# Hymba diffusion step on one core: an earlier gate row, a PSUM tile for each half of tile 8's last columns, separate norms of tiles 6 and 7, and a one-input softmax maximum

## Chip, cores and metric

The kernel runs on one core of one Trainium2 chip. The time is the device time in microseconds of one execution of the program; a kernel's time is the median of its runs. Engines are named as in the profile: PE (TensorE, matmuls), PEld (its weight loads), DVE (VectorE), ACT (ScalarE), POOL (GpSimd), SP (SyncE, which here issues DMAs). DMAs are issued from the queues of SP, ACT and POOL.

## What is computed

One step of a hybrid trunk with one layer, D = 1024, for 1024 latent tokens (with 256 cached context keys) and a prompt of 128 tokens. Cut to what matters here:

```python
def _block_attention(q_nope, q_ropes, key_sets):          # per head, per 128 query rows
    ...
        s = jnp.concatenate(logits, axis=-1).astype(jnp.float32) * ATTN_SCALE   # 1024 latent + 256 context keys
        p = jax.nn.softmax(s, axis=-1)
        return jnp.einsum('bhqk,bkhv->bqhv', p, v_all)

def _back(x, gate, a_out, attn, g_b, w_o):
    y = jnp.concatenate([a_out, attn * jax.nn.silu(g_b)], axis=-1) @ w_o
    return x + gate * y

    y_prompt = _rmsnorm(xp, final_g)
    y_sample = _rmsnorm(xs, final_g)
```

The mixer's other group (a gated MLP) and the input projections lie ahead of this and are not touched.

## The kernel before

Rows are worked on in nine tiles of 128: tiles 0 to 7 are the latent tokens, tile 8 the prompt. A product in fp32 is made of three matmuls on split numbers: each operand x has a rounded part (hi) and the rest x - hi (lo). The hi block is a copy with a cast on ACT or POOL, the lo block a subtraction on DVE (`lo_of`, L112).

**Attention.** For each tile t and head h, `softmax(t, h, ...)` takes the row maximum m over the 1024 latent logits (L1481) and over the 256 context logits (L1484), makes `nb`, the bias of the exponential, as max times `nscl` (L1485), the exponentials on ACT (L1491), and 1/sum (L1495, L1496); POOL multiplies (L1497). `value_stream` then works in steps of 512 columns: PE transposes e into `pT` (L1558), ACT writes its hi part `ph` (L1562), DVE its lo part `pl` (L112), and PE adds three matmuls each into `o` (L1582 to L1584); ACT copies `o` (L1592), PE multiplies by the value weights (`at`, L1601), DVE multiplies into `mixB` (L1603). Each engine runs its instructions in program order. `later(d, fn)` puts a piece of work d microseconds of an estimated clock later in that order.

**Work that rides along.** The output weights W_o are split (`wo_piece`), and weight sums T1 to T4 are formed in 16 `units`, each with a POOL subtraction of `traw` (L809), and stored to DRAM. The lists `his` and `los` hold split jobs, of which `spare_hi` and `spare_lo` issue a few after each softmax head and each `pl`. `t_fetch(3, n, ...)` loads the four T3 blocks back from DRAM (from POOL's queue, into the memory of split weights); `early_split(2)` issues the split of the third ring block, ringC; `wo_need(k)` issues whatever the k-th weight block still needs.

**Output projection.** Latent tiles go in pairs (0,1), (2,3), (4,5), (6,7), each a 2x2 block product in Strassen-Winograd form: seven products A11, A12, A22 and S1 to S4, with right sides B11, B21, B22, T1 to T4. Their left operands lie in rings of hi and lo blocks, ringA (in `area`), ringB and ringC. Three products of the first pair, in PSUM banks f0, f1, f2, and the prompt's right 512 columns (w8) are begun during the last attention heads (`early`); what is left of them is in `rest`. PE then goes through the products in the order S2, S3, S1, A11, ... (`products`). DVE combines their banks: c11, then m11, the multiplication of the first pair's columns by the gate row (L2195), u2, u4 and so on.

**The last part's order** is written by `Plan`, a list scheduler: steps have an engine, a cost, a priority (low first), what they wait for, and what they take and give back (PSUM banks "w", raw tiles). `fetch` chains loads one behind the other, cost 1.35. `load_gate` (L2048) loads the latent gate row as 128x1024, `load_own` the prompt's, `load_xr` (L1991) the residual x. For each group of tiles `norm` makes the sum of squares, a square root, a reciprocal with a correction, and the scaling by final_g: tile 6 on DVE (L2120), tile 7 in halves on POOL (L2132) and ACT (L2128). Last comes tile 8's left half: `left` makes columns 0 to 256 and 256 to 512 in one PSUM tile (`pz0`, `pz1`, 24 matmuls each); for each half DVE multiplies by the gate (`zm`, L2273) and adds x (`za`, L2274), ACT squares (`sq8.0`, `zq`), then follow zv, the root zr, rlast, and the output scaling: `out0` (DVE, left columns, SP's queue) and `out1` (ACT, right columns, ACT's queue).

Of the kernel before, what the change touches and what calls it, by code (L numbers as in the profile page):

```python
# [9 lines left out]
F32 = mybir.dt.float32  # L10
# [3 lines left out]
AF = mybir.ActivationFunctionType  # L14
ALU = mybir.AluOpType
# [3 lines left out]
P = 128  # L19
# [75 lines left out]
def tile_hymba_step(ctx: ExitStack, tc: tile.TileContext, I, O):  # L95
# [1375 lines left out]
    def softmax(t, h, lat_, con_):  # L1471

        m = sm.tile([P, 2], F32, tag="m", name=f"m{t}{h}", bufs=3)
        nb = sm.tile([P, 1], F32, tag="nb", name=f"nb{t}{h}", bufs=3)
        su = sm.tile([P, 2], F32, tag="su", name=f"su{t}{h}", bufs=3)
        rs = sm.tile([P, 1], F32, tag="rs", name=f"rs{t}{h}", bufs=3)
        e = ap_.tile([P, 1280], F32, tag="e", name=f"e{t}{h}", bufs=6)
        es[t, h] = e

        def start():  # L1480
            V.tensor_reduce(m[:, 0:1], lat_, axis=AX.X, op=ALU.max)  # L1481

        def shift():
            V.tensor_reduce(m[:, 1:2], con_, axis=AX.X, op=ALU.max)  # L1484
            V.scalar_tensor_tensor(nb, m[:, 0:1], m[:, 1:2], nscl[:, t : t + 1], op0=ALU.max, op1=ALU.mult)  # L1485
# [298 lines left out]
    with tc.manual_schedule(engines=engines):  # L1784
# [208 lines left out]
        def plain(k):  # L1993
            out_terms(8, wps[8], 512, 1024, [k])
            if k == 3:
                at_ = sum(1 for fn in his if rank.get(fn, 1) < 1)
                his[at_:at_] = [lambda n=n: t_fetch(3, n, woh[n][:, 512:1024], wol[n][:, 512:1024]) for n in range(4)]

        early = [(0.65, lambda k=k: plain(k)) for k in range(4)]
        early += [(0.65, lambda k=k: product(0, first_banks[0], ks=[k])) for k in range(4)]  # L2000
# [1 line left out]
            early.append((0.65, lambda k=k: plain(4 + k)))  # L2002
            early.append((0.65, lambda k=k: product(1, first_banks[1], ks=[k])))
        early += [(0.65, lambda k=k: product(2, first_banks[2], ks=[k])) for k in range(3)]
        later(6.0, lambda: (wo_need(4), early_split(2)))
        later(2.0, lambda: [t_piece(2, n, flat[2][2 + n]) for n in range(4)])
        vs = value_stream(pairs[-2])
        merged(vs[:3], [])
# [38 lines left out]

    def load_gate():  # L2048
        gate[0] = ep.tile([P, 1024], F32, name="gate0", tag="gate0")
        nc.scalar.dma_start(  # L2050
            gate[0].rearrange("p (j r) -> p j r", j=4), gdram.rearrange("j (c r) -> c j r", c=2)[0:1].broadcast_to([P, 4, 256])
        )

# [2 lines left out]
    def load_own(i, dma):  # L2056
# [2 lines left out]
        dma(t_[:, 0:512].rearrange("p (j r) -> p j r", j=2), rows.broadcast_to([P, 2, 256]))  # L2059
        dma(t_[:, 512:1024], I["x"][8][:, 512 * i : 512 * i + 512])  # L2060

    for m, n in ((1, 0), (4, 4)):
        for k in range(4):
            fetch(f"T{m}{k}", lambda m=m, k=k, n=n: t_piece(m, k, tpiece[n + k]))
        if m == 1:
            fetch("gate0", load_gate)
    fetch("own1", lambda: load_own(1, nc.scalar.dma_start))
    for t in (0, 1):
        fetch(f"x{t}", lambda t=t: load_xr(t))
# [7 lines left out]
        used[0] += n  # L2077
        return smalls[:, c : c + n]

    groups = {t: g for g in ((8,), (0, 1), (2, 3), (4, 5), (6, 7)) for t in g}  # L2080

    def square(t, j, junk, c, deps, prio=3.0, src=None):
        g = groups[t]
# [91 lines left out]
    def pair(n):  # L2175
# [24 lines left out]
        if True:  # L2200
# [56 lines left out]
    def finish_left():  # L2257
        v, v0, root, u = (small(1) for _ in range(4))
        r = sm.tile([P, 1], F32, tag="fr", name="rlast")
        cell = {}  # L2260
        fetch("own0", lambda: load_own(0, nc.sync.dma_start), ["y4"])
        g, x = (lambda: own[0][:, 0:512]), (lambda: own[0][:, 512:1024])
        on_g("z4", lambda: G.tensor_tensor(keep, keep, fg[:, R], op=ALU.mult), ["sq8.1", "fg"], 2.5)

        def left(j, c):
            if j == 0:
                cell["o"] = psw.tile([P, 512], F32, tag="w", name="left")
                cell["junk"] = psw.tile([P, 512], F32, tag="w", name="junk")
            out_terms(8, cell["o"][:, c], c.start, c.stop, range(8))

        for j, c in enumerate((slice(0, 256), slice(256, 512))):
            on_t(f"pz{j}", 2.9, lambda j=j, c=c: left(j, c), [], takes=("w", "w") if j == 0 else ())
            on_v(f"zm{j}", lambda c=c: V.tensor_tensor(cell["o"][:, c], cell["o"][:, c], g()[:, c], op=ALU.mult), [f"pz{j}", "own0"], 0.5, 0.42)  # L2273
            on_v(f"za{j}", lambda c=c: V.tensor_tensor(cell["o"][:, c], cell["o"][:, c], x()[:, c], op=ALU.add), [f"zm{j}"], 0.5, 0.42)  # L2274
        square(8, 0, lambda: cell["junk"][:, 0:256], L, ["za0"], 0.5, lambda: cell["o"][:, 0:256])
        sums((8,), v0, 0.5)
        on_v("zv1", lambda: V.tensor_scalar(v0, v0, 1.0 / 1024.0, EPS, op0=ALU.mult, op1=ALU.add), ["n8"], 0.5, 0.16)
        on_s(
            "zq", lambda: S.activation(cell["junk"][:, 256:512], cell["o"][:, 256:512], AF.Square, accum_out=ssq[(8,)][:, 2:3]), ["za1"], 0.4, 0.6
        )  # L2280
        on_v("zv", lambda: V.scalar_tensor_tensor(v, ssq[(8,)][:, 2:3], 1.0 / 1024.0, v0, op0=ALU.mult, op1=ALU.add), ["zq", "zv1"], 0.4, 0.2)
        on_s("zr", lambda: S.activation(root, v, AF.Sqrt), ["zv"], 0.3, 0.25)
        on_v("zr0", lambda: V.reciprocal(r, root), ["zr"], 0.3, 0.18)
        on_v("zr1", lambda: V.scalar_tensor_tensor(u, v, -0.5, r, op0=ALU.mult, op1=ALU.mult), ["zr0"], 0.3, 0.18)
        on_v("zr2", lambda: V.tensor_tensor(u, u, r, op=ALU.mult), ["zr1"], 0.3, 0.18)
        on_v("zr3", lambda: V.scalar_tensor_tensor(r, u, 1.5, r, op0=ALU.add, op1=ALU.mult), ["zr2"], 0.3, 0.18)

        def out0():
            V.scalar_tensor_tensor(x(), cell["o"], r, fg[:, L], op0=ALU.mult, op1=ALU.mult)
            nc.sync.dma_start(O["y"][8][:, L], x())  # L2290
# [116 lines left out]
```

## Time and profile before

| | |
|---|---|
| runs (us) | 624.31, 625.5, 625.46; median 625.46 |
| the profiled execution | 624.43 us, of it 622.7 us of span |
| granted TensorE clock, mean | 0.989 |
| PE, DVE, ACT, POOL busy | 96%, 69%, 53%, 34% |
| DMA | 67.33 MB, 108 GB/s over the span |

The span is the time from the profile's first instruction to its last. The page gives busy time by engine, the chain of work that ended last, and groups of instructions by line; a row of the timeline is start, duration, engine, line, operation, `out<-in`, shape, and in brackets the idle time before it with what ended it. A duration of a DVE row overlaps the next row's start by about 0.08 us; matmul durations include the way through the array, so the distance between starts is what one costs. A row of waits is who waited for whom: us in total, times, longest. In a row of the chain stand start, duration and what ran. DMA groups give KB of each transfer and the median us from issue to landing.

### The profile page before, as it was taken

Reading aid. Unit: us, or ns where it says so; the run is one execution under the profiler, and the core shown is the slowest. Engines: PE = TensorE matmul, PEld = TensorE weight load, DVE = VectorE, ACT = ScalarE, POOL = GpSimd, SP = SyncE. Lnnn points to the kernel's source line nnn. Section 1 sums busy time; section 2 is a strip of 40 time slices with the busy share of each in tenths; the row PEclk is TensorE's granted clock in tenths of the full one; section 3 lists DMA queues with packets and bytes.
Section 4 is the critical chain, followed back from the end, with each engine's and each line's share of the span. In section 5 each row is a group of like instructions: output and inputs, shape, how many; then the busy total and the mean of one; then the engine's idle time right before and its main releaser. Section 6 shows DMA issues by size and latency. Waiting matters only on the chain.

```text
span 622.7 us, 10205 instructions
## 1 busy us (share of the span) xinstructions
PE 599.6 (96%) x3671; PEld 540.6 (87%) x3671; DVE 427.5 (69%) x909; ACT 329.6 (53%) x763; POOL 209.2 (34%) x254
## 2 busy tenths in 40 slices
PE   7999999999999999999999999999999999799992
PEld 7678889999989999999988998899999888588882
DVE  4683458897755567566778677768777755368874
ACT  6556754336423345455676556665655542456642
POOL 2561111000000000333363354535344565179721
PEclk8999999999999999999999999999999999989997
DMA  8992010101261044000020143334411056932442
GB/s 321 390 376 69 1 34 2 35 1 54 100 237 65 21 119 131 14 1 1 2 74 1 35 136 121 126 128 135 133 72 35 1 201 196 369 113 77 157 139 101
DMA packets 32082, 67.33 MB, mean 108 GB/s; under 512 B 3472, under 2 KB 18592, under 8 KB 31520
## 3 DMA queue, kind: packets, MB, share of 16 engines
q1 hardware_dynamic: 27344, 54.88, 25.5%
q0 software_dynamic: 2880, 8.39, 4.1%
q10 hardware_dynamic: 1808, 3.41, 1.6%
q8 instruction: 29, 0.48, 0.3%
q14 instruction: 21, 0.17, 0.1%
HBM read 53.45 MB, written 13.21 MB: 107 GB/s over the span
## 4 chain that ended last, share of the span: by engine, by line
PE 80%; DVE 10%; ACT 4%; DMA 3%; issue 2%; SPq 0%; ACTq 0%
PE p L954 10%; PE tp L752 8%; PE tp L976 5%; PE pT L1558 4%; DVE pl L112 3%; PE zacc L1390 2%; PE zacc L1389 2%; PE zacc L1391 2%; PE s L1512 2%; PE s L1514 2%; PE s L1513 2%; PE s L1511 2%; PE s L1515 2%; DMA gate<-gdram 2%; PE o L1584 2%
## 5 line engine op out<-in xcount | busy, mean ns | idle before, releaser
L1497 POOL TENSOR_SCALAR e<-e,rs 128x1280 f32<-128x1280 f32 x32 | 46.9, 1466 | 100.4 <-ACT ph L1562 60.4
L112 DVE TENSOR_TENSOR pl<-pT,ph 128x512 fp32r<-128x512 f32 x81 | 55.4, 687 | 36.2 <-ACT ph L1562 34.5
L1491 ACT ACTIVATE e<-s,nb,scl 128x256 f32<-128x256 f32 x64 | 56.1, 880 | 41.0 <-DVE nb L1485 41.0
L1562 ACT CAST ph<-pT 128x512 fp32r<-128x512 f32 x80 | 46.3, 587 | 35.6 <-PE pT L1558 34.0
L1237 POOL TENSOR_TENSOR kr<-z,rope 128x64 f32<-128x64 f32 x8 | 2.6, 323 | 171.9 <-ACT z L1246 171.9
L752 PE MATMUL tp<-area,w 128*128 128x384 f32 x288 | 52.5, 338 | 0.0
L1558 PE MATMUL pT<-ident,e 128*128 128x128 f32 x320 | 48.4, 274 | 3.3 <-DVE pl L112 3.1
L752 PEld LDWEIGHTS tp<-area,w 128*128 128x128 f32 x288 | 50.4, 188 | 0.4
L1582 PE MATMUL o<-ph,vh 128*128 128x256 f32 x160 | 47.6, 298 | 0.0
L1584 PE MATMUL o<-ph,vl 128*128 128x256 f32 x160 | 45.0, 281 | 0.0
L1583 PE MATMUL o<-pl,vh 128*128 128x256 f32 x160 | 45.0, 281 | 0.0
L1558 PEld LDWEIGHTS pT<-ident,e 128*128 128x128 f32 x320 | 37.0, 140 | 8.1 <-PE at L1601 2.8
L1481 DVE TENSOR_REDUCE m<-s 128x1 f32<-128x1024 f32 x32 | 38.9, 1217 | 1.5 <-PE s L1515 1.5
L1511 PE MATMUL s<-kch,area 128*128 128x512 f32 (+2 forms) x100 | 39.1, 391 | 0.0
L1512 PE MATMUL s<-kcl,area 128*128 128x512 f32 (+2 forms) x100 | 35.3, 353 | 0.0
L1514 PE MATMUL s<-krh,area 128*128 128x512 f32 (+2 forms) x100 | 35.3, 353 | 0.0
L1513 PE MATMUL s<-kch,area 128*128 128x512 f32 (+2 forms) x100 | 35.2, 352 | 0.0
L1515 PE MATMUL s<-krl,area 128*128 128x512 f32 (+2 forms) x100 | 35.2, 352 | 0.0
L976 PE MATMUL tp<-area,w 128*128 128x384 f32 x192 | 35.0, 337 | 0.0
L976 PEld LDWEIGHTS tp<-area,w 128*128 128x128 f32 x192 | 33.6, 188 | 0.4 <-issue 0.4
L1583 PEld LDWEIGHTS o<-pl,vh 128*128 128x128 f32 x160 | 30.2, 189 | 1.4
L1582 PEld LDWEIGHTS o<-ph,vh 128*128 128x128 f32 x160 | 30.1, 188 | 1.4
(664 smaller groups left out, 1726.9 us busy)
## 6 DMA issues: line engine op xcount, KB each, us to landing
ada<-in_ada_ss SPq DMA_DIRECT2D x16, 512.0 KB, 8.1
w2r<-in_w_t SPq DMA_DIRECT2D x12, 512.0 KB, 4.4
x<-in_x SPq DMA_DIRECT2D x9, 512.0 KB, 7.2
adag<-in_ada_g SPq DMA_DIRECT2D x4, 1024.0 KB, 4.8
traw<-in_w_o SPq DMA_DIRECT2D x16, 256.0 KB, 3.7
tdram<-thi SPq DMA_DIRECT2D x32, 128.0 KB, 1.9
tdram<-traw SPq DMA_DIRECT2D x32, 128.0 KB, 1.9
wor<-in_w_o SPq DMA_DIRECT2D x8, 512.0 KB, 4.1
```

The lines of the kernel that those rows point to most:

```text
L112: V.tensor_tensor(lo, src, f32(hi), op=ALU.subtract)
L752: T.matmul(tps[i, g][:, :GW], w_[i][:, k, :], x_[k, g], start=k == 0 and j == 0, stop=k == NK - 1 and j == 2)
L954: T.matmul(banks[key], a_, b_, start=k == 0 and m == 0, stop=k == 3 and m == len(passes) - 1)
L976: T.matmul(tps[c, 2][:, :GW], w_[c][:, k, :], x_[k, 2], start=k == 0 and m == 0, stop=k == NK - 1 and m == 2)
L1491: S.activation(e[:, sl], src, AF.Exp, bias=nb, scale=scl[:, t : t + 1], accum_out=su[:, i : i + 1])
L1511: T.matmul(ps, qh_, kch[:, sl], start=True, stop=False)
L1512: T.matmul(ps, qh_, kcl[:, sl], start=False, stop=False)
L1514: T.matmul(ps, qr_, krh[:, sl], start=False, stop=False)
L1558: T.transpose(ps[:, w : w + P], es[t, h][:, c * P : (c + 1) * P], ident)
L1582: T.matmul(o, vh[:, kt, :], ph[:, sl], start=c == 0, stop=False)
L1583: T.matmul(o, vh[:, kt, :], pl[:, sl], start=False, stop=False)
L1584: T.matmul(o, vl[:, kt, :], ph[:, sl], start=False, stop=c == n - 1)
```

## The change

Four edits. (1) The reduction to `nb` has one input: a `tensor_reduce` over both columns of m and a `tensor_scalar` in place of a `scalar_tensor_tensor`, while `units` or `his` still hold work; that is so for 20 of the 32 heads. (2) The gate row is the first fetch of the last part and goes to SP's queue; the T3 loads go to the end of `his`, and `early_split(2)` is due at 0.5 instead of 6.0, without `wo_need(4)`. (3) Tiles 6 and 7 are two groups with norms of their own, at priority 0.45. (4) The two halves of tile 8's left columns have a PSUM tile each, and `out0` is two operations.

```diff
@@ softmax, shift() @@
-            V.scalar_tensor_tensor(nb, m[:, 0:1], m[:, 1:2], nscl[:, t : t + 1], op0=ALU.max, op1=ALU.mult)
+            if units or his:
+                V.tensor_reduce(nb, m, axis=AX.X, op=ALU.max)
+                V.tensor_scalar(nb, nb, nscl[:, t : t + 1], None, op0=ALU.mult)
+            else:
+                V.scalar_tensor_tensor(nb, m[:, 0:1], m[:, 1:2], nscl[:, t : t + 1], op0=ALU.max, op1=ALU.mult)
@@ plain(k) @@
             if k == 3:
-                at_ = sum(1 for fn in his if rank.get(fn, 1) < 1)
-                his[at_:at_] = [lambda n=n: t_fetch(3, n, woh[n][:, 512:1024], wol[n][:, 512:1024]) for n in range(4)]
+                his.extend([lambda n=n: t_fetch(3, n, woh[n][:, 512:1024], wol[n][:, 512:1024]) for n in range(4)])
@@ last attention heads @@
-        later(6.0, lambda: (wo_need(4), early_split(2)))
+        later(0.5, lambda: early_split(2))
@@ load_gate and the order of fetches @@
-        nc.scalar.dma_start(
+        nc.sync.dma_start(
+    fetch("gate0", load_gate)
     for m, n in ((1, 0), (4, 4)):
         for k in range(4):
             fetch(f"T{m}{k}", lambda m=m, k=k, n=n: t_piece(m, k, tpiece[n + k]))
-        if m == 1:
-            fetch("gate0", load_gate)
@@ norms @@
-    groups = {t: g for g in ((8,), (0, 1), (2, 3), (4, 5), (6, 7)) for t in g}
+    groups = {t: g for g in ((8,), (0, 1), (2, 3), (4, 5), (6,), (7,)) for t in g}
-            norm((a, b), 1.5)
+            for g in dict.fromkeys((groups[a], groups[b])):
+                norm(g, 0.45 if n == 3 else 1.5)
@@ finish_left @@
         def left(j, c):
+            cell[j] = psw.tile([P, 512], F32, tag="w", name=f"left{j}")
             if j == 0:
-                cell["o"] = psw.tile([P, 512], F32, tag="w", name="left")
                 cell["junk"] = psw.tile([P, 512], F32, tag="w", name="junk")
-            out_terms(8, cell["o"][:, c], c.start, c.stop, range(8))
+            out_terms(8, cell[j][:, H], c.start, c.stop, range(8))
...
-            on_t(f"pz{j}", 2.9, lambda j=j, c=c: left(j, c), [], takes=("w", "w") if j == 0 else ())
+            on_t(f"pz{j}", 2.9, lambda j=j, c=c: left(j, c), [], takes=("w",) if j else ("w", "w"))
...
-            V.scalar_tensor_tensor(x(), cell["o"], r, fg[:, L], op0=ALU.mult, op1=ALU.mult)
+            for j in range(2):
+                c = slice(256 * j, 256 * j + 256)
+                V.scalar_tensor_tensor(x()[:, c], cell[j][:, H], r, fg[:, c], op0=ALU.mult, op1=ALU.mult)
```

The lines left out read the halves from the new tiles. Behind the fourth line of `shift` line numbers grow by two to eight.

How the order of instructions moves. On SP, at the end of attention, before (wor is a row block of W_o, xr a tile of x):

```order
L1654 DMA wor_5769<-in_w_o 128x1024
L1654 DMA wor_5771<-in_w_o 128x1024
L1991 DMA xr_6202<-in_x 128x1024
L1991 DMA xr_6208<-in_x 128x1024
L2121 DMA out_y<-xr_6157 128x1024
```

The same place of SP after the change:

```order
L1658 DMA wor_5789<-in_w_o 128x1024
L1658 DMA wor_5791<-in_w_o 128x1024
L2053 DMA gate_6074<-gdram 128x4x256
L1995 DMA xr_6222<-in_x 128x1024
L1995 DMA xr_6228<-in_x 128x1024
L2123 DMA out_y<-xr_6177 128x1024
```

The gate row is in SP's order now, between the last weight block and the first x tile of the second pair.

On DVE, from the last `pl` block of attention to the first combinations, before:

```order
L806 TENSOR_TENSOR f_5775<-f_5775,mixA 128x512
L112 TENSOR_TENSOR ringC<-mixB,ringC 128x512
L112 TENSOR_TENSOR pl_4_6003<-pT_4_5997,ph_4_6002 128x512
L1603 TENSOR_TENSOR mixB<-mixB,at_6032 128x2x128
L112 TENSOR_TENSOR area_118<-raw_6067,area_118 128x512
L112 TENSOR_TENSOR ringB<-raw_6074,ringB 128x512
L112 TENSOR_TENSOR ringC<-raw_6090,ringC 128x512
L806 TENSOR_TENSOR mixA<-S_0_6076,mixA 128x4x128
L112 TENSOR_TENSOR area_118<-raw_6112,area_118 128x512
L2195 TENSOR_TENSOR mixB<-f_5775,gate_6094 128x4x128
L112 TENSOR_TENSOR ringB<-raw_6132,ringB 128x512
```

The same place of DVE after the change (`f` is c11, `mixB<-f,gate` is m11):

```order
L112 TENSOR_TENSOR pl_4_6017<-pT_4_6011,ph_4_6016 128x512
L1607 TENSOR_TENSOR mixB<-mixB,at_6048 128x2x128
L806 TENSOR_TENSOR f_5795<-f_5795,mixA 128x512
L112 TENSOR_TENSOR area_118<-raw_6088,area_118 128x512
L2197 TENSOR_TENSOR mixB<-f_5795,gate_6074 128x4x128
L112 TENSOR_TENSOR ringB<-raw_6095,ringB 128x512
L112 TENSOR_TENSOR ringC<-raw_6112,ringC 128x512
L806 TENSOR_TENSOR mixA<-S_0_6098,mixA 128x4x128
L112 TENSOR_TENSOR area_118<-raw_6133,area_118 128x512
L112 TENSOR_TENSOR ringB<-raw_6152,ringB 128x512
```

c11 moved behind the last `at`, ringC's first lo block out of this stretch to the middle of the last tile's attention, and m11 from behind the lo blocks of area, ringB, ringC and area to a place behind the first of them.

On PE, from the next-to-last `o` matmul block to the last block's transposes, before:

```order
L1584 MATMUL o_5830<-ph_1_5923,vl 128x256
L1919 MATMUL f_5775<-area_120,ringB 128x512
L1920 MATMUL f_5775<-area_120,ringB 128x512
L1921 MATMUL f_5775<-area_120,ringB 128x512
L1948 MATMUL w_5773<-area_120,area_118 128x512
L1949 MATMUL w_5773<-area_120,area_118 128x512
L1919 MATMUL f_5776<-area_119,ringC 128x512
L1920 MATMUL f_5776<-area_119,ringC 128x512
L1950 MATMUL w_5773<-area_120,ml_5456 128x512
L1921 MATMUL f_5776<-area_119,ringC 128x512
L1558 MATMUL pT_4_5997<-ident,e_5649 128x128
```

On PE after the change, from the last product of f2's third block to the first of S2 (the `o` matmuls and transposes now follow `f_5796<-area_119,ringC` directly):

```order
L1925 MATMUL f_5796<-krh_5787,ringC 128x512
L1605 MATMUL at_6048<-os_6046,wuv 128x128 x2
L1923 MATMUL f_5795<-area_120,ringB 128x512
L1924 MATMUL f_5795<-area_120,ringB 128x512
L1925 MATMUL f_5795<-area_120,ringB 128x512
L1952 MATMUL w_5793<-area_120,area_118 128x512
L1953 MATMUL w_5793<-area_120,area_118 128x512
L1954 MATMUL w_5793<-area_120,ml_5472 128x512
L1923 MATMUL f_5796<-area_120,ringC 128x512
L1924 MATMUL f_5796<-area_120,ringC 128x512
L1925 MATMUL f_5796<-area_120,ringC 128x512
L1923 MATMUL S_0_6098<-area_120,area_118 128x512
```

The last three matmuls of f1 and of w8 moved from ahead of the last block's transposes to behind `at`.

More of the change, by code (lines that the diff above doesn't have):

```diff
@@ L2263, in finish_left @@
         on_g("z4", lambda: G.tensor_tensor(keep, keep, fg[:, R], op=ALU.mult), ["sq8.1", "fg"], 2.5)
+        H = slice(0, 256)
         def left(j, c):
+            cell[j] = psw.tile([P, 512], F32, tag="w", name=f"left{j}")
             if j == 0:
-                cell["o"] = psw.tile([P, 512], F32, tag="w", name="left")
                 cell["junk"] = psw.tile([P, 512], F32, tag="w", name="junk")
-            out_terms(8, cell["o"][:, c], c.start, c.stop, range(8))
+            out_terms(8, cell[j][:, H], c.start, c.stop, range(8))
         for j, c in enumerate((slice(0, 256), slice(256, 512))):
-            on_t(f"pz{j}", 2.9, lambda j=j, c=c: left(j, c), [], takes=("w", "w") if j == 0 else ())
-            on_v(f"zm{j}", lambda c=c: V.tensor_tensor(cell["o"][:, c], cell["o"][:, c], g()[:, c], op=ALU.mult), [f"pz{j}", "own0"], 0.5, 0.42)
-            on_v(f"za{j}", lambda c=c: V.tensor_tensor(cell["o"][:, c], cell["o"][:, c], x()[:, c], op=ALU.add), [f"zm{j}"], 0.5, 0.42)
-        square(8, 0, lambda: cell["junk"][:, 0:256], L, ["za0"], 0.5, lambda: cell["o"][:, 0:256])
+            o = lambda j=j: cell[j][:, H]
+            on_t(f"pz{j}", 2.9, lambda j=j, c=c: left(j, c), [], takes=("w",) if j else ("w", "w"))
+            on_v(f"zm{j}", lambda o=o, c=c: V.tensor_tensor(o(), o(), g()[:, c], op=ALU.mult), [f"pz{j}", "own0"], 0.5, 0.42)
+            on_v(f"za{j}", lambda o=o, c=c: V.tensor_tensor(o(), o(), x()[:, c], op=ALU.add), [f"zm{j}"], 0.5, 0.42)
+        square(8, 0, lambda: cell["junk"][:, 0:256], L, ["za0"], 0.5, lambda: cell[0][:, H])
         sums((8,), v0, 0.5)
@@ L2278, in finish_left @@
         on_s(
-            "zq", lambda: S.activation(cell["junk"][:, 256:512], cell["o"][:, 256:512], AF.Square, accum_out=ssq[(8,)][:, 2:3]), ["za1"], 0.4, 0.6
+            "zq", lambda: S.activation(cell["junk"][:, 256:512], cell[1][:, H], AF.Square, accum_out=ssq[(8,)][:, 2:3]), ["za1"], 0.4, 0.6
         )
```

## Prediction

> **What bounds the kernel now.** I read the page's engine shares first, then its chain, then the waits, and went to single rows only where a wait stands on a line of the diff. The page:
>
> ```profile
> span 622.7 us, 10205 instructions
> PE 599.6 (96%) x3671; PEld 540.6 (87%) x3671; DVE 427.5 (69%) x909; ACT 329.6 (53%) x763; POOL 209.2 (34%) x254
> ...
> PE 80%; DVE 10%; ACT 4%; DMA 3%; issue 2%; SPq 0%; ACTq 0%
> ```
>
> TensorE is busy for 96% of the span, and the diff takes no matmul out of it (it shifts six). So the change can win only where PE waits, or where PE has finished. DMA's 3% of the chain leads to one transfer. Here it is in the list of waits, in the chain and on PE's timeline, and below it the busy time of stretches:
>
> ```profile
> DVE mixB L2195 <- DMA gate<-gdram: 7.0, 1, 7.0
> 531.56 11.19 DMA gate<-gdram
> 543.61 0.47 PE L1919 MATMUL A<-area 128*128 128x512 f32 x1 [3.96 <-DVE mixB L2195]
> ```
>
> ```profile
> core 0: us, PE busy (x) PEld busy (x) DVE busy (x) ACT busy (x) POOL busy (x), PEclk, DMA share, GB/s
> 526.00:536.00 10.00, 10.00 (x57) 8.36 (x56) 4.39 (x7) 4.74 (x9) 5.60 (x9) 1.00 0.93 312
> 540.00:545.00 5.00, 1.39 (x6) 1.14 (x7) 2.19 (x4) 0.72 (x2) 0.00 (x0) 0.97 1.05 348
> 545.00:550.00 5.00, 5.00 (x17) 4.02 (x16) 4.17 (x7) 1.77 (x4) 4.53 (x4) 0.69 0.53 202
> ```
>
> The gate row takes 11.2 us from its issue (531.56) to its use (542.8); DVE waits 7.0 us for it, and PE 3.96. The stall costs more than itself: the granted clock of the 5 us behind it is 0.69, which at half speed or full makes 3.1 us at half speed, a loss of 1.6 us. The second place is the last 11 us: PE ends at 611.67 (its last row is under term 3), the span at 622.7. The third is small: PE waits 0.2 us at a transpose (pT), once for each of seven pairs of softmax heads.
>
> **Term 1, the gate row.** It moves from ACT's queue, behind the T1 blocks, to SP's, first in its order: by the rows under "The change" behind the last weight row (wor) and ahead of an xr load. Its tile lies in the memory of softmax blocks, so it waits for their last reader, an `o` matmul of the last block. That one now runs earlier, since six matmuls (f1 and w8, last k) go behind `at`.
>
> ```profile
> 525.53 0.50 PE L1921 MATMUL f<-area,ringC 128*128 128x512 f32 x1 [0.25 <-DVE ringC L112]
> 525.87 0.60 PE L1558 MATMUL pT<-ident,e 128*128 128x128 f32 x4
> 529.01 0.28 PE L1584 MATMUL o<-ph,vl 128*128 128x256 f32 x1
> 530.99 0.40 PE L1919 MATMUL S<-area,area 128*128 128x512 f32 x1
> ...
> 539.03 0.40 PE L1920 MATMUL S<-tp,ringC 128*128 128x512 f32 x1
> 539.26 0.40 PE L1921 MATMUL S<-tp,ringC 128*128 128x512 f32 x1
> ```
>
> ```profile
> 543.38 0.68 DVE L112 TENSOR_TENSOR ringB<-raw,ringB 128x512 fp32r<-128x512 f32 x1
> 526.65 3.25 POOL L1915 DMA_DIRECT2D tp<-tdram  x6 [3.40 <-PE pT L1558]
> 529.20 0.33 SPq L1991 DMA_DIRECT2D xr<-in_x  x1
> wor<-in_w_o SPq DMA_DIRECT2D x8, 512.0 KB, 4.1
> ```
>
> Six matmuls, 0.23 us apart as the two rows at 539 are, make 1.4; with ringC's 0.25 wait (its lo block now comes much earlier) and 0.2 of start behind that wait, the last block's pT comes 1.9 us earlier, at 524.0. The last `o` ends at 529.29 - 1.9 = 527.4, and the gate can issue at 527.45, 4.1 us before 531.56. S2 starts only some 0.5 us earlier (530.5), since the six matmuls still stand ahead of it.
>
> How long is the way from issue to use? At most as before, 11.2 us: use at 538.65. At best as one of SP's loads of the same 512 KB, 4.1 us and 0.5 to the use: 532.0. The DMA share is 0.93 and 1.05 through the old transfer's time, and the same blocks go by in the new one; only the xr load of 529.20 (512 KB at 348 GB/s, 1.5 us), which was ahead, is now behind, and part of it had gone already. The old row is much the nearer: I take 10.2 us, use at 537.7, and keep 535.5 to 538.65 as this term's own bounds.
>
> Now what is queued behind that wait. Before, m11 (the multiplication by the gate) stood behind the lo blocks of area, ringB, ringC and area; now it stands ahead of the last three of these. S3, PE's second product, needs that ringB block for its third matmul. So PE stops after S2 and two matmuls, at 533.7, and no longer after S1 (539.66). From the gate's use: m11 0.6, the ringB block 0.7 and 0.15 of start bring S3 back; 22 matmuls of S3 and S1 at 0.23 are 5.1. A starts 6.5 us behind the use, at 544.2 against 543.61. **Term 1: +0.6 us**; the bounds give -1.6 (535.5) and +1.5 (538.65). Break-even is a use at 537.1, 9.65 us behind the issue. The stall becomes 5.4 us long instead of 4, so the slow clock behind it stays in the sum as it is.
>
> Of what else moves here I count nothing: POOL's copy for ringC and three T3 loads go ahead of T2's, in an engine that idles 3.4 us at 526.65; the own and xr loads on ACT's queue fall behind the stall, to about 545 from 540, and their users run on POOL and DVE beside PE's products (1 to 2 us if PSUM banks come free too late).
>
> **Term 2, the softmax maximum.** In 20 of 32 heads one DVE operation with two columns of m becomes a reduction and a multiplication by a pointer. Rows of the timeline, then three rows of single lines (ns: least, median, most):
>
> ```profile
> 359.66 1.55 POOL L809 TENSOR_TENSOR traw<-traw 128x256 f32<-128x256 f32 x2
> 359.01 1.22 DVE L1481 TENSOR_REDUCE m<-s 128x1 f32<-128x1024 f32 x1
> 360.14 0.42 DVE L1484 TENSOR_REDUCE m<-s 128x1 f32<-128x256 f32 x1
> 360.59 0.64 DVE L1485 SCALAR_TENSOR_TENSOR nb<-m,nscl 128x1 f32<-128x1 f32 x1
> 361.15 0.68 DVE L112 TENSOR_TENSOR pl<-pT,ph 128x512 fp32r<-128x512 f32 x1
> 361.98 0.63 PE L1558 MATMUL pT<-ident,e 128*128 128x128 f32 x4 [0.21 <-DVE pl L112]
> 366.72 0.22 DVE L1485 SCALAR_TENSOR_TENSOR nb<-m,nscl 128x1 f32<-128x1 f32 x1
> 434.96 0.64 DVE L1485 SCALAR_TENSOR_TENSOR nb<-m,nscl 128x1 f32<-128x1 f32 x1
> ```
>
> ```profile
> L1701 DVE TENSOR_SCALAR nb<-m,nscl x1: 229/229/229, 320.3 to 320.3; 128x4 f32<-128x4 f32 x1
> L1213 DVE TENSOR_SCALAR zv<-ssz x18: 144/154/155, 246.7 to 308.4; 128x1 f32<-128x1 f32 x18
> L393 DVE TENSOR_SCALAR x<-x,x3r x4: 740/756/1007, 10.7 to 38.2; 128x1024 f32<-128x1024 f32 x4
> ```
>
> The old operation takes 0.22 us alone and 0.64 where it starts under a POOL subtraction of traw; it then ends with it (359.66 + 1.55 = 361.21). That is so in seven of the 20 heads, 12.4 us apart, from 360.59 to 434.96, each with a late pl and a waiting pT. For the new pair: from 1024 to 256 columns a reduction falls by 1.04 ns a column, so two columns take about 0.15 us; the multiplication has L1701's 0.23; with a gap the pair is 0.41 long, and its successor, which starts 0.08 before the end of the one ahead, comes 0.33 behind the pair's start. Against 0.56 that frees 0.235 us in an obstructed head; against 0.14 it costs 0.19 in a free one. The free head between two obstructed ones (366.72) lies on the path too: its exponential waits for it, and from there DVE runs without a gap to the next obstructed one. Seven times 0.235 - 0.19: **term 2 is -0.35 us.** The ends: -1.65 if only the gain counts (7 x 0.235), +1.3 if only the cost does (7 x 0.19).
>
> The Trainium skill, "SBUF — State Buffer", section "Who interferes with whom", speaks against the second half of the pair: a reduction never contends with GpSimd, but a tensor_scalar can enter a two-port mode, and then one of the two blocks for the other's whole instruction. By that rule the obstructed heads would keep their end and term 2 would be +1.3. The rows here are split: 18 multiplications of one column ran in 144 to 155 ns, while one of four of 1024 columns was stretched to 1007. I go by the small ones.
>
> **Term 3, the end.**
>
> ```profile
> 608.95 1.28 POOL L2132 TENSOR_TENSOR xr<-xr,fg 128x512 f32<-128x512 f32 x1 [0.82 <-ACT A L2089]
> 611.39 0.28 PE L1950 MATMUL left<-area,ml 128*128 128x256 f32 x1
> 611.71 0.43 DVE L2273 TENSOR_TENSOR left<-left,own 128x256 f32<-128x256 f32 x1 [3.59 <-PE left L1950]
> 613.87 1.27 DVE L2120 SCALAR_TENSOR_TENSOR xr<-xr,fss,fg 128x1024 f32<-128x1024 f32 x1
> 615.07 0.42 DVE L2273 TENSOR_TENSOR left<-left,own 128x256 f32<-128x256 f32 x1
> 617.83 0.75 DVE L2289 SCALAR_TENSOR_TENSOR own<-left,rlast,fg 128x512 f32<-128x512 f32 x1
> 618.61 0.33 SPq L2290 DMA_DIRECT2D out_y<-own  x1
> ```
>
> Tile 8's last columns are made in two halves in one PSUM tile, and DVE's work on the first half waits 3.59 us for the second, up to 611.71. Then the norm of tiles 6 and 7, tile 6's scaling (1.27) and the second half (615.07) follow one another. With a tile for each half the first starts when its 24 matmuls are through (half as wide, so 0.12 apart): 611.67 - 2.9 = 608.8. Tile 6's norm no longer waits for 7's, and its scaling runs under PE's second half, from 609.4 to 611.5 if POOL's multiplication of 608.95 holds it up. The second half then comes at 612.05, 3.0 us before 615.07. Not all of that stays: ACT's scaling of tile 7 (0.72) and a DMA issue (0.35) now stand ahead of the last square root. zq at 613.0, root 614.65, rlast 615.6, out0 in two halves to 616.4, the last issue, on ACT's queue, at 616.7 against 618.61. **Term 3: -1.9 us**, from -2.5 (the root ahead of the scaling) to -1.2 (the six added norm operations of 0.12 us on the path too).
>
> **Sum.** 0.6 - 0.35 - 1.9 = -1.65 us. The profiled execution took 624.43 us, near the low end of the runs shown (624.31 to 625.5, median 625.46). I start half of that 1.03 us above it, at 624.95, and get 623.3.
>
> **Rivals.**
> - *The gate comes in time.* If 5 us do from issue to use, m11 is through before ringB's block is due at 532.5, and the stall (3.96) and its slow clock (1.6) go: 623.3 - 0.6 - 5.6 = 617.1. For it speaks the 4.1 of SP's loads, against it the full DMA queues. Chance 0.12.
> - *The wait is moved and longer: slower.* It now stands ahead of S3's ringB block, and every us beyond a use at 537.1 is one of PE's. From 539.35 on (11.9 us behind the issue, 0.7 more than before) it eats terms 2 and 3. With 14 us, because block loads that went out earlier are in front, term 1 is +4.3 and the time 627.0. For it speaks that 11.2 us were needed among the same neighbours, against it that the gate now goes ahead of xr. Chance 0.15.
> - *The softmax edit does not do what it says:* the multiplication is held up under POOL as its predecessor was, term 2 is +1.3, and the sum 0.0: 624.95. Chance 0.17.
> - *It does all of it:* term 2 is -1.65, and the time 622.0. Chance 0.12.
>
> **How the numbers follow.** The forecast, 621.5 to 624.8 by its terms' bounds, has 0.44. The range of 619.5 to 626.8 leaves out the gate in time (0.12) and about half of its opposite (0.075). A measurement of this kernel tells 0.2%, 1.25 us, from no change. Faster by more, under 624.2: the first and the fourth rival and 0.36 of the forecast, 0.60. Slower by more, over 626.7: the upper part of the second rival, and its meeting with the third, 0.15. Between them 0.25.
>
> **What would show it.** Term 1: the gate's issue near 527.5 on SP's queue, DVE waiting for it ahead of ringB's block, a hole of 5 us in PE after two matmuls of S3 and none ahead of A. No hole, with a granted clock of 1 from 540 to 550, is the first rival, a hole of 8 us the second. Term 2: pairs of 0.4 us under POOL's subtractions too, and pT waits that shrink but do not all go; a multiplication of 0.4 us or more there is the third rival. Term 3: the first half's DVE row near 609, under PE, and 9 us from PE's end to the span's instead of 11. Likeliest to be wrong is the gate's time on the way, which no row of before shows in the new place.

## The result and the profile after

The changed kernel takes 626.59 us (median of 19 runs, 624.62 to 628.68), the kernel before 626.01 us beside it (19 runs, 624.31 to 628.59). The ratio is 1.0008 with a 95% interval of 0.9996 to 1.002: no change that can be told from none. Forecast was 1.65 us less. The profiled execution of the changed kernel took 625.82 us, 1.39 more than that of before. Its page:

```profile
span 624.0 us, 10238 instructions
PE 599.9 (96%) x3671; PEld 540.1 (87%) x3671; DVE 428.7 (69%) x936; ACT 329.7 (53%) x765; POOL 207.8 (33%) x254
...
PE 76%; DVE 11%; DMA 5%; ACT 4%; issue 2%; SPq 0%; ACTq 0%; DVEq 0%
```

PE's work is the same and its share of the chain is smaller, 76% instead of 80%, while DMA's grew from 3% to 5%. Where that comes from stands in the list of waits, in the chain and on the timelines of SP, DVE and PE:

```profile
DVE mixB L2197 <- DMA gate<-gdram: 8.9, 1, 8.9
528.55 11.91 DMA gate<-gdram
528.55 0.38 SPq L2053 DMA_DIRECT2D gate<-gdram  x1
540.55 0.69 DVE L2197 TENSOR_TENSOR mixB<-f,gate 128x512 f32<-128x512 f32 x1 [8.87 <-DMA gate<-gdram]
541.16 0.68 DVE L112 TENSOR_TENSOR ringB<-raw,ringB 128x512 fp32r<-128x512 f32 x1
541.90 0.80 PE L1925 MATMUL S<-area,ringB 128*128 128x512 f32 x1 [6.98 <-DVE ringB L112]
542.50 0.63 PE L1923 MATMUL S<-area,ringB 128*128 128x512 f32 x1
549.09 0.40 PE L1923 MATMUL A<-area 128*128 128x512 f32 x1
```

The hole in PE is where it was expected, at the third matmul of S3, with none ahead of A. But it is 6.98 us long where 5.4 were forecast, and the hole before was 3.96. The gate needs 12.0 us from its issue (528.55) to its use (540.55). The stretches show what follows (columns as in the prediction: length, busy time by engine, granted clock, DMA share, GB/s):

```profile
536.00:540.00 4.00, 0.00 (x0) 0.00 (x0) 0.00 (x0) 0.00 (x0) 0.00 (x0) 0.93 1.12 397
540.00:545.00 5.00, 3.10 (x7) 2.48 (x8) 3.08 (x5) 0.59 (x1) 0.00 (x0) 0.50 0.42 157
545.00:550.00 5.00, 5.00 (x20) 4.00 (x19) 1.38 (x2) 1.73 (x3) 0.00 (x0) 0.87 0.01 2
```

For 4 us no engine does anything while DMA is full. The granted clock is at half from 539.42 to 546.25, and 4.4 us of that fall on matmuls. For all kernels of this study the span can be cut at the same five marks: the first `at` of the stage with pairs, its fourteenth, the first matmul of S2, the first of A11 of the second pair, and PE's last. Each column is the time from one mark to the next (us, one profiled execution each):

```
kernel            at1-at14  at14-S2  S2-A    A-PE's end  PE's end-span's end
before            159.20    22.62    12.62   68.06       10.99
the change        159.41    22.09    17.51   66.47        8.40
tail_only         159.25    22.64    12.71   68.80        8.40
softmax_only      159.57    22.60    12.84   68.08       10.79
gate_only         159.25    22.13    18.18   66.46       10.99
gate_late_mul     159.49    22.13     9.18   66.44        8.40
softmax_seven     157.48    22.59    12.32   67.90       10.98
gate_4k           159.42    22.55    14.03   66.36        8.40
before_4k         159.22    22.59     8.83   66.44       11.00
all_mended        157.52    22.58     8.25   66.36        8.61
fetch_only        159.29    22.62    18.71   66.36       10.99
t3_only           159.27    22.10    11.79   67.93       10.99
norms_only        159.26    22.63    12.88   68.08       11.21
halves_only       159.26    22.61    12.87   68.05        7.91
t4_behind         159.50    22.57    12.70   80.20        8.36
mended_one_norm   157.60    22.11     8.25   66.90        7.90
```

Between the first two rows: +0.21, -0.53, +4.89, -1.59 and -2.59, together +0.4. The rest of the two spans' 1.3 us lies ahead of the first `at`, which came at 349.17 and 350.07. That first part, in which the inputs come in, differs from run to run (349.2 to 351.5 in the kernels that are alike there; the four with 4 KB gate rows store these rows in it, and reached that mark at 349.9 to 352.3), so the table compares what comes behind it.

### The profile page after: what moved, and what is told of

It reads as the page before. It is cut to its first block, busy times and chain, and to the rows that moved or that the text cites. A ratio compares the mean times of both kernels' runs of the same rounds, so it can differ in the third digit from the quotient of the medians.

```text
span 624.0 us, 10238 instructions
## 1 busy us (share of the span) xinstructions
PE 599.9 (96%) x3671; PEld 540.1 (87%) x3671; DVE 428.7 (69%) x936; ACT 329.7 (53%) x765; POOL 207.8 (33%) x254
## 4 chain that ended last, share of the span: by engine, by line
PE 76%; DVE 11%; DMA 5%; ACT 4%; issue 2%; SPq 0%; ACTq 0%; DVEq 0%
PE p L954 10%; PE tp L752 8%; PE tp L976 5%; DVE pl L112 4%; PE pT L1562 3%; DVE m L1481 2%; PE zacc L1390 2%; PE zacc L1391 2%; PE zacc L1389 2%; ACT e L1495 2%; PE S L1925 2%; PE S L1923 2%; PE S L1924 2%; DMA gate<-gdram 2%; DMA ada<-in_ada_ss 2%
```

## Experiments

Times are medians, with the ratio to the kernel before on the same chip and its interval; what a name contains is in its diff. The diffs are cut to their main lines. Unless another base is named, the base is the kernel before. The rows shown are of one profiled execution of each kernel.

**tail_only: the last two edits alone** (groups (6,) and (7,), a tile for each half, out0 in two).

```diff
+    groups = {t: g for g in ((8,), (0, 1), (2, 3), (4, 5), (6,), (7,)) for t in g}
+            for g in dict.fromkeys((groups[a], groups[b])):
+                norm(g, 0.45 if n == 3 else 1.5)
+            cell[j] = psw.tile([P, 512], F32, tag="w", name=f"left{j}")
```

> The kernel before with edits 3 and 4 alone (norms of 6 and 7 apart, a PSUM tile for each half, out0 in two). Theory: the end is shortened by itself; from PE's end to the span's end 8.4 us instead of 11.0, so about 2.5 us faster than before. Rival: the end got shorter only because PE came late at it and the norm work had caught up; then PE's end stays where it was and the gain is under 1 us.

624.18 us, 0.996 (0.9945 to 0.9975). The end is 2.6 us shorter by itself; PE's end did not have to come late for it. The theory holds.

**softmax_only: the maximum alone.**

```diff
+            if units or his:
+                V.tensor_reduce(nb, m, axis=AX.X, op=ALU.max)
+                V.tensor_scalar(nb, nb, nscl[:, t : t + 1], None, op0=ALU.mult)
```

> The kernel before with edit 1 alone. Theory: the pair frees 0.05 us in each of seven pairs of heads and loses about 0.7 us in five later heads in which the old operation was hardly held up: between -0.1 and +0.4 us in all. Rival: the pairs' gain is all there is, -0.35 us, and the losses in the later heads come from edit 2.

626.01 us, 0.9999 (0.9985 to 1.0012): nothing. Its trace has +0.37 us from the first to the fourteenth `at`. In it the seven pairs gain 0.3 us and the later heads lose 0.7, and they do so without the edit at the T3 loads.

**gate_only: the gate on SP's queue and first of the fetches, T3 loads last, ringC's split early.**

```diff
-        later(6.0, lambda: (wo_need(4), early_split(2)))
+        later(0.5, lambda: early_split(2))
-        nc.scalar.dma_start(
+        nc.sync.dma_start(
+    fetch("gate0", load_gate)
```

> The kernel before with edit 2 alone. Theory: the gate row's wait stands ahead of the ringB block that S3 needs; PE stops for 7 us after two matmuls of S3, and the kernel is 2.5 to 3 us slower than before. Rival: the loss seen in the whole change comes from another edit (softmax heads) or from the start; then within 1 us of before.

629.39 us, 1.0031 (1.0014 to 1.0048), about 2 us slower (0.9 to 3.0 by the interval). From S2 to A it has 18.18 us instead of 12.62, with PE's hole, 7.62 us, at the same matmul. This edit is the loss.

**gate_late_mul: the whole change, with m11 ordered behind the lo block of the seventh ring block.** Only the order of DVE changes: m11 stands behind four lo blocks again.

```diff
-            on_v(D_("m11"), lambda: V.tensor_tensor(C, ps("A12"), gL(), op=ALU.mult), [D_("c11"), "gate0", f"hi{at_['S2']}", f"raw{at_['S2']}"], 2, gives=("w",))
+            on_v(D_("m11"), lambda: V.tensor_tensor(C, ps("A12"), gL(), op=ALU.mult), [D_("c11"), "gate0", f"hi{at_['S2']}", f"raw{at_['S2']}", *(["lo6"] if n == 0 else [])], 2, gives=("w",))
```

> The whole change, with m11 made to wait for the lo block of the seventh ring block (area), so that DVE's order around the gate is again that of before. Theory (the place of the wait is the loss): the gate's load takes its 12 us as it did, but PE works through S2, S3 and S1 under it and stops 1 to 1.5 us ahead of A, with no slow clock behind it: 7 to 8 us faster than the whole change, about 619. Rival (the load's time is the loss, wherever the wait stands): A starts where it does in the whole change, and the time stays within 2 us of it.

618.8 us, 0.9877 (0.9857 to 0.9897). Rows of its chain, of DVE and of PE:

```profile
528.08 11.35 DMA gate<-gdram
539.45 0.69 DVE L2197 TENSOR_TENSOR mixB<-f,gate 128x512 f32<-128x512 f32 x1 [3.82 <-DMA gate<-gdram]
540.29 0.47 PE L1923 MATMUL A<-area 128*128 128x512 f32 x1 [0.78 <-DVE mixB L2197]
```

The load still takes 11.4 us, and PE stands still for 0.78 us instead of 6.98; no stretch at half clock follows it. So the place of the wait in DVE's order is what turns the load's time into PE's.

**fetch_only and t3_only: the two parts of the gate edit.** The first has the new queue and the new place among the fetches, the second the two lines at the T3 loads and at ringC's split.

```diff
 fetch_only
-        nc.scalar.dma_start(
+        nc.sync.dma_start(
+    fetch("gate0", load_gate)
 t3_only
+                his.extend([lambda n=n: t_fetch(3, n, woh[n][:, 512:1024], wol[n][:, 512:1024]) for n in range(4)])
+        later(0.5, lambda: early_split(2))
```

> The kernel before with the gate on SP's queue and first of the fetches, without the two edits at the T3 loads and ringC. Theory (first in the fetches is what puts m11 ahead of ringB's lo block): m11 stands ahead of it here too; the last softmax block is read 1.9 us later than in the whole edit 2, so the gate issues at about 529.5 and the stall in S3 is near 8 us: 4 to 5 us slower than before. Rival (the T3 part of edit 2 makes the loss): within 1 us of before.

> The kernel before with the T3 loads last in their list and ringC's split early, and the gate as it was. Theory: the ringC wait goes and S2 starts 0.5 us earlier, the gate's stall ahead of A takes most of it back: 0 to 0.5 us faster. Rival (the T3 part of edit 2 makes the loss): 2 us or more slower.

fetch_only: 631.58 us, 1.008 (1.0054 to 1.0107), 5 us slower, with a hole of 8.41 us at the same matmul; in DVE's order m11 stands ahead of ringB's lo block in it, and in t3_only behind four lo blocks as before. t3_only: 623.39 us, 0.9965 (0.9949 to 0.9982), about 2.2 us faster, more than was expected of it: its trace has 0.52 us less ahead of S2 and 0.83 less from S2 to A, where the gate, still on ACT's queue, needs 10.8 us from issue to use. The rest of the 2.2 us is not seen in that one execution. So the loss comes with the new queue and the new place among the fetches. That it is the place, by which the scheduler puts m11 ahead, and not the queue is not shown by a run with the queue alone; gate_late_mul, which keeps both and moves m11 back, has no such loss.

**gate_4k and before_4k: larger packets.** The two gate rows are kept in DRAM as two rows of 1024, so that the broadcast reads 4 KB for each partition and not four times 1 KB; the first on the whole change, the second on the kernel before.

```diff
-    gdram = gd.tile([4, 512], F32, tag="gdram", name="gdram")
+    gdram = gd.tile([2, 1024], F32, tag="gdram", name="gdram")
-            gate[0].rearrange("p (j r) -> p j r", j=4), gdram.rearrange("j (c r) -> c j r", c=2)[0:1].broadcast_to([P, 4, 256])
+            gate[0], gdram[0:1, :].broadcast_to([P, 1024])
```

> The whole change, with the gate rows stored in DRAM as two rows of 1024, so that the broadcast reads 4 KB at a time and not 1 KB. Theory (the queues are served packet by packet in turn, so a transfer of 512 small packets gets a quarter of what one of 4 KB packets gets): the gate is on its way 2.5 to 3 us instead of 6.5, m11 starts 8 us behind the issue instead of 12, PE's stall in S3 shrinks to about 3 us and the slow clock behind it goes: 4 to 6 us faster than the whole change, 621 to 622.5. Rival (the bytes ahead of it set its time): no change beyond 1 us.

> The kernel before with that storage of the gate rows alone. Theory: the gate arrives about 4 us earlier, just when S1 ends, and both the 4 us stall and the slow clock behind it go: 5 to 6 us faster, near 620.5. Rival: as above, no change beyond 1 us.

gate_4k: 621.58 us, 0.9928 (0.9903 to 0.9954), 5.0 under the whole change, with a hole of 3.91 us in S3; the slow clock behind it did not go, as the theory had it, but halved to 3.41 us. Its trace is of the slowest of its six executions, 624.83 us, with the first `at` at 352.3; behind that mark it is 3.1 us shorter than the whole change's. before_4k: 619.99 us, 0.9903 (0.9884 to 0.9922), 6.4 under the kernel before, a little more than expected. The packets' size sets much of the load's time. m11 in gate_4k, then m11 and A in before_4k:

```profile
540.13 0.69 DVE L2197 TENSOR_TENSOR mixB<-f,gate 128x512 f32<-128x512 f32 x1 [5.80 <-DMA gate<-gdram]
```

```profile
539.93 0.69 DVE L2195 TENSOR_TENSOR mixB<-f,gate 128x512 f32<-128x512 f32 x1 [3.17 <-DMA gate<-gdram]
540.77 0.47 PE L1919 MATMUL A<-area 128*128 128x512 f32 x1
```

In the first the issue was at 531.20, so 8.9 us to the use instead of 12.0. In the second it was at 532.51, 7.4 us instead of 11.2, and A starts behind S1 without a wait worth a row.

**t4_behind: the whole change, with 2 MB of the blocks that travel beside the gate sent later.** The T4 loads go behind POOL's first block sum in POOL's order.

```diff
-            fetch(f"T{m}{k}", lambda m=m, k=k, n=n: t_piece(m, k, tpiece[n + k]))
+            fetch(f"T{m}{k}", lambda m=m, k=k, n=n: t_piece(m, k, tpiece[n + k]), ["s01"] if (m, k) == (4, 0) else [])
```

> The whole change with the four T4 loads (2 MB, POOL's queue) behind POOL's first block sum, so that only the T1 loads stand beside the gate row. Theory (the blocks beside it set the gate's time): 8 to 9 us from the gate's issue to m11 instead of 12, PE's stall in S3 3 to 4 us instead of 7; a new wait for the late T4 blocks may eat a part of it. Rival (the 512 small packets or the way before the first of them set it alone): 11.3 us or more, the stall as it was.

635.62 us, 1.0155 (1.0129 to 1.0182), two runs. As a kernel it is a loss, since POOL comes to the T4 loads too late; PE waits 9.5 us for them in four places, of which the first is shown, and a stretch of 13.65 us at half the granted clock begins among them, at 555.66:

```profile
529.15 7.49 DMA gate<-gdram
536.73 0.69 DVE L2197 TENSOR_TENSOR mixB<-f,gate 128x512 f32<-128x512 f32 x1 [4.45 <-DMA gate<-gdram]
538.07 0.50 PE L1925 MATMUL S<-area,ringB 128*128 128x512 f32 x1 [2.58 <-DVE ringB L112]
551.37 0.48 PE L1923 MATMUL A<-tp,ringC 128*128 128x512 f32 x1 [0.90 <-DMA tp<-tdram]
```

As a measurement it decides: 7.6 us from issue to use, and a hole of 2.58 us in S3, both a little under what the theory gave, and far from the rival. The trace's packets in single microseconds say how (gate packets are of 1 KB, in gate_4k of 4 KB, those of POOL's queue of 4 KB):

```
kernel       microsecond   gate packets   POOL's packets
the change   536 to 537    84             76
t4_behind    533 to 534    80             68
t4_behind    534 to 535    297            15
gate_4k      537 to 538    43             42
```

Beside the blocks, the gate gets about one packet for each of theirs, whatever its size; nearly alone, 1 KB packets go at 297 a microsecond. The Trainium skill, "DMA: Bandwidth & Descriptors", section "Queues, rings and completion order", says that a DMA engine goes round the queues in turn and drains a whole packet, typically about 9 to 17 descriptors, from one before it switches. The even counts agree with such turns; whether the records counted here are packets in that sense, they do not show.

**softmax_seven: the two-operation maximum only in the seven heads in which the old operation ran under POOL's subtraction of traw.**

The diff is against the changed kernel's line; all else is as in the kernel before.

```diff
-            if units or his:
+            if units and t >= 2 and h % 2 == 0:
```

> The kernel before with the two-operation maximum in the seven heads alone whose old operation ran under a POOL subtraction of traw. Theory (a port lock that the pair escapes, and a fixed price of 0.19 us where there was no lock): each of the seven pairs of heads gets 0.235 us shorter, no later head changes, 1.6 us faster than before. Rival (the free head of a pair sets the pace, whatever the obstructed one costs): under 0.5 us faster.

624.79 us, 0.9971 (0.9959 to 0.9983). From the first to the fourteenth `at` it takes 157.48 us, 1.72 less than before: the whole gain of the seven heads, and nothing given back in the others. PE's waits for pl, in the kernel before's seven pairs 0.2 us each, are gone from them. Here the first of the seven, under a POOL subtraction:

```profile
360.23 1.56 POOL L809 TENSOR_TENSOR traw<-traw 128x256 f32<-128x256 f32 x2
361.16 0.15 DVE L1486 TENSOR_REDUCE nb<-m 128x1 f32<-128x2 f32 x1
361.35 0.21 DVE L1487 TENSOR_SCALAR nb<-nb,nscl 128x1 f32<-128x1 f32 x1
361.48 0.68 DVE L112 TENSOR_TENSOR pl<-pT,ph 128x512 fp32r<-128x512 f32 x1
362.30 0.63 PE L1562 MATMUL pT<-ident,e 128*128 128x128 f32 x4
```

**norms_only and halves_only: the two parts of the end.** (Diff: of tail_only the first three lines, with their priority 0.45, or the last.)

> The kernel before with the norms of 6 and 7 apart, both halves in one PSUM tile. Theory (each part undoes one wait): DVE still waits for PE's end with the first half, which stands ahead of tile 6's scaling; the scaling starts at 612.4 instead of 613.9 on the scale of before, about 1.2 us faster. Rival (the norm's order is the whole gain): 2.5 us.

> The kernel before with a PSUM tile for each half, and one norm for 6 and 7. Theory: the first half no longer holds up DVE, so the common norm and tile 6's scaling run under PE's second half too, and the gain is nearly that of both parts, 2 to 2.5 us. Rival (it takes both): under 1 us.

norms_only: 626.93 us, 1.0014 (0.9998 to 1.003), no gain, and by its trace an end of 11.21 us against 10.99: both expectations missed. halves_only: 622.11 us, 0.9944 (0.9925 to 0.9964), more than expected, with an end of 7.91 us, shorter than with both parts. POOL's multiplication for tile 7 and DVE's scaling of tile 6 beside it, in the changed kernel (with its last root) and in halves_only:

```profile
612.84 1.28 POOL L2134 TENSOR_TENSOR xr<-xr,fg 128x512 f32<-128x512 f32 x1 [0.87 <-ACT A L2091]
613.40 1.81 DVE L2122 SCALAR_TENSOR_TENSOR xr<-xr,fss,fg 128x1024 f32<-128x1024 f32 x1
618.20 0.16 ACT L2288 ACTIVATE smalls<-smalls 128x1 f32<-128x1 f32 x1 [0.43 <-ACT xr L2130]
```

```profile
609.23 1.28 POOL L2132 TENSOR_TENSOR xr<-xr,fg 128x512 f32<-128x512 f32 x1 [0.82 <-ACT A L2089]
609.11 0.43 DVE L2276 TENSOR_TENSOR left<-left,own 128x256 f32<-128x256 f32 x1 [0.71 <-PE left L1950]
611.28 1.28 DVE L2120 SCALAR_TENSOR_TENSOR xr<-xr,fss,fg 128x1024 f32<-128x1024 f32 x1
612.47 0.43 DVE L2276 TENSOR_TENSOR left<-left,own 128x256 f32<-128x256 f32 x1
614.26 0.16 ACT L2285 ACTIVATE smalls<-smalls 128x1 f32<-128x1 f32 x1 [0.23 <-DVE smalls L2284]
```

With the common norm, the scaling comes late enough to miss POOL's multiplication (1.28 us instead of 1.81), ACT is done with both of tile 7's scalings when the last root is due, and the root comes 2.3 us behind PE's end (611.95) instead of 2.6. The halves are the gain; the separate norms, with the priority that came with them, cost.

**all_mended and mended_one_norm.** m11 behind the lo blocks, 4 KB gate rows, the two-operation maximum in seven heads and the rest of the change; the second with the common norm of 6 and 7. (Diffs as above, on the whole change.)

> The whole change with m11 behind the lo blocks, 4 KB gate rows, and the two-operation maximum in the seven heads alone. Theory: to the 618.8 of the one with m11 behind come 0.8 us of stall ahead of A and about 1.9 us of softmax: 616 to 616.5. Rival: the stall at A was all that the gate still cost, and softmax gives nothing: 618.

> The kernel with m11 behind the lo blocks, 4 KB gate rows, the two-operation maximum in seven heads and a PSUM tile for each half, but with the common norm of tiles 6 and 7 as before the change. Theory (the halves bring the whole gain at the end, the separate norms cost 0.2 to 0.5 us): the end from PE's last matmul takes 8.0 us instead of 8.6, and the time is 616 to 616.5, 0.5 us under the one with separate norms. Rival (with PE ended earlier the norms matter): 0.5 us over it.

all_mended: 616.85 us, 0.9875 (0.9831 to 0.9919), a little over what was expected, with six executions from 614.79 to 622.67. mended_one_norm: 614.37 us, 0.9818 (0.9801 to 0.9836), 11.6 us under the kernel before by the medians and 1.6 under the expected range. Its page, and its row of m11:

```profile
span 612.6 us, 10216 instructions
PE 598.1 (98%) x3671; PEld 539.7 (88%) x3671; DVE 428.8 (70%) x917; ACT 329.6 (54%) x763; POOL 207.8 (34%) x254
```

```profile
534.36 0.69 DVE L2197 TENSOR_TENSOR mixB<-f,gate 128x512 f32<-128x512 f32 x1 [0.28 <-DMA gate<-gdram]
```

From S2 on PE has no wait at all. The separate norms cost here too: the ends are 7.90 and 8.61 us, as expected. Behind the first `at` the two traces differ by 0.6 us in all. The medians differ by 2.5, but they come from different chips and all_mended's executions are 8 us apart, so the 2.5 is no measure of the norms.

## Why the prediction was wrong

**The frame was right.** PE's work bounds the kernel, and the change moved time only at the three places named. The places came as said: the gate's issue lay 3.03 us ahead of S2's first matmul (531.58 - 528.55; forecast 530.5 - 527.45), the hole at S3's third matmul, pairs of 0.4 us that POOL does not hold up, the end shortened under PE's second half.

**Term 1 failed, at the step "I take 10.2 us, use at 537.7".** Measured are 12.0 us. The bounds of the term, 535.5 to 538.65, took the old 11.2 us as the most that the way could need, on the ground that the xr load was now behind the gate instead of ahead. That saved nothing. By the traces' DMA records the gate's first packet came 3.70 us behind the issue before the change, with xr ahead, and 3.95 after it, with xr behind; the packets then took 6.66 us and 7.49, and from the last one to the use it was 0.86 and 0.56. What the gate shares its way with are POOL's blocks, and it gets about one 1 KB packet for one 4 KB packet of theirs while they go by (gate_4k, before_4k and t4_behind each took one side of that away, and the time went from 12.0 to 8.9, from 11.2 to 7.4, and from 12.0 to 7.6). In the earlier place it met more of them: 546 packets of the blocks went out during its own, 479 before. In gate_only, fetch_only and gate_late_mul, with the same place among the fetches, the way was 12.6, 12.3 and 11.4 us. What holds back the first packet is left open.

The same step's rest, that the slow clock "stays in the sum as it is", was too low by about half a microsecond: the clock was at half for 3.41 us in the kernel before and for 6.83 in the changed one, of which the last 4.4 us fell on matmuls. The Trainium skill, "TensorE: Matmul & The Clock Gate", section "Part 1: The HAM clock gate (the "warmup" mystery)", gives a free-running window of 3413 ns; the two stretches are one and two of these. In sum term 1 is -0.53 + 4.89 - 1.59 = +2.8 us instead of +0.6: 1.8 from the way, 0.5 from the clock.

The second rival described this: the wait is one of PE's for each microsecond beyond the break-even, and eats terms 2 and 3 from 11.9 us behind the issue on. It came out at 12.0. It was priced with 14 us, at 627.0, and given 0.15; the only gate row of the trace, 11.2 us among the same neighbours, spoke for it more than for 10.2.

**Term 2 had the right mechanism and left out a cost.** The seven pairs gave 0.45 us (from the first to the ninth `at` the stretch went from 98.78 to 98.33), against 0.35 forecast (seven times 0.045 are 0.32). The pair's durations were right, and none of its 20 multiplications was stretched. Below them, a wait at pT that stayed in one of the seven pairs, and two in later heads that are new:

```profile
L1487 DVE TENSOR_SCALAR nb<-nb,nscl x20: 212/214/216, 349.1 to 497.1; 128x1 f32<-128x1 f32 x20
362.82 0.41 PE L1562 MATMUL pT<-ident,e 128*128 128x128 f32 x2 [0.16 <-DVE pl L112]
485.54 0.41 PE L1562 MATMUL pT<-ident,e 128*128 128x128 f32 x2 [0.26 <-DVE pl L112]
498.06 0.30 PE L1562 MATMUL pT<-ident,e 128*128 128x128 f32 x1 [0.32 <-DVE pl L112]
```

So the third rival is out. The Trainium skill, "SBUF — State Buffer", section "Who interferes with whom", by which a tensor_scalar can enter a two-port mode and then contend with GpSimd, ties this to conditions on the operands; at one column it was not held up in any of the seven heads (212 to 215 ns under POOL's subtraction). The later heads, whose losses I left out of the sum, cost 0.66 us (60.42 to 61.08 us from the ninth to the fourteenth `at`). The step that failed is "-0.35" as the sum of the seven pairs alone; with the later heads the term is +0.21. softmax_seven showed the other side: without the cost in the free heads the gain is 1.72, near the -1.65 given as the end.

**Term 3 was right in its main part and took credit for the wrong half.** The end got 2.6 us shorter, forecast was 1.9 and at most 2.5. From PE's end to the last root it took 2.64 us (615.56 to 618.20) where 2.98 was worked out. But "tile 6's norm no longer waits for 7's" was counted as a help; by the ends of norms_only, halves_only and mended_one_norm, the separate norms with their new priority cost 0.2 to 0.7 us, and the PSUM tile for each half gives 3.1.

So the sum that was to be -1.65 is 2.8 + 0.2 - 2.6 = +0.4 us by the traces, beside +0.6 by the medians. Of the 3.3 us between the forecast time, 623.3, and the measured one, 1.1 come from its starting level of 624.95, where the kernel before has 626.01.

## What to carry to other kernels

When a load is issued earlier, look whether its first user moves ahead of other work: an instruction that waits for a load holds everything behind it in its engine's order, and here four positions in DVE's order were worth 7 to 8 us. Price a transfer by the stream that it enters, packet for packet, and make the packets of the one that is waited for large. An operation that another engine does not hold up, but that costs more by itself, belongs only where the old one is held up.

## What the runs showed of the hardware that was not expected

- Turns between DMA queues go by packets: 84 packets of 1 KB beside 76 of 4 KB in a microsecond, 43 beside 42 where both had 4 KB, 297 of 1 KB once the other queue was nearly empty (15 packets).
- The length of a stall alone did not set the stretch at half the granted clock: around the gate's wait it was 3.41 us for holes of 2.58 us (t4_behind) to 4.22, and 6.83 for those of 6.98 to 8.41, but also for one of 4.04 in tail_only (its 68.80 us in the table). None followed the 0.78 us of gate_late_mul.
- The first packet of the gate row came 3.5 to 4.0 us behind its issue in all sixteen kernels, with 1 KB and with 4 KB packets, on ACT's queue and on SP's.
- The input stage, ahead of the first `at`, took between 349.2 and 351.5 us in executions of the same code; differences under 3 us between two single executions are therefore read behind it.
